# Unread TensorE products in front of the first merge's products and behind the scores of ten half units

## The chip, the cores and the metric

The kernel runs on one core of one Trainium2 chip. The metric is the device time of one execution in microseconds (us), lower is better. A core has TensorE (PE; the load of its stationary operand is listed apart, as PEld), VectorE (DVE), ScalarE (ACT), GpSimd (POOL) and queues that issue DMAs; SyncE's (SP) is the one used most here. Each engine works through its own queue in order; semaphores make one engine wait for another or for a DMA.

## The reference

One layer of a hybrid diffusion backbone on 1024 latent tokens and 256 context tokens of width 1024, in float32. What matters here, cut short:

```python
h  = rmsnorm(x, g_pre) * (1 + scale) + shift              # adaLN, likewise hc for the context
na_q, na_k, na_v, na_z, g_qkv, g_z, g_b, g_a = split(h @ w_in)
o_na = neighborhood_attention(...)                        # 8 heads, windows of 8 x 16 on a 16 x 64 grid, plus all context keys
...
# gated DeltaNet, 4 heads, both directions, in chunks:
a     = where(i > j, (kb @ k.T) * decay, 0)
t_inv = triangular_solve(eye + a, eye)                    # unit lower triangular inverse
u, w  = t_inv @ (v * beta), t_inv @ (kb * exp(gc))
state, o = scan(step, state0, ...)
y = concat(o_na * silu(na_z), o_g * silu(g_z)) @ w_out
x = x + gate * rmsnorm(y, g_post)
```

## The kernel before

Every projection `h @ w_in` is done as three products of rounded halves (`hh`, `hl` for the tokens, `wh`, `wl` for the weights), each 128 x 512 and eight deep in the width. A product that goes to a gate is called `pz` (lines L603, L607 and L608 of `mm_chan`), one that goes to a query or a key `pq` or `pk`. ScalarE and VectorE take the sum out of PSUM (`st_z` for a gate, L703 and L704) and SyncE's queue stores it (`z_dram`).

The triangular inverses of the DeltaNet chunks (128 x 128 per chunk, head and direction) are made in two steps. VectorE inverts the 32 x 32 diagonal blocks by substitution (`ab_vv`, L1255 and L1258) and they go to DRAM (`yd`). Then `inv_merge`, once per head, loads these blocks (`vl<-yd`, four DMAs) and the off-diagonal parts (`pmf<-pm_dram`, two DMAs, one per direction, `pm[0]` and `pm[1]` in the code), turns them with three transposes on VectorE in a row (`vx`, `vd`, `ld`, L1291 to L1293), and joins blocks of 32 to 64 and of 64 to 128 by small products on TensorE. The first of these small products of a head are the 40 of 32 x 32 for each stage named `tz` (L1305): they need `ld` and `pmf`. They are followed by `tu` (L1324), then 64 x 64 products (L1338, L1344, L1346), and the merged inverse goes to DRAM (`tm_dram`, L1351). There are two buffers of `vl`, and one `tm` buffer (`self.tms[2]`) serves every head in turn.

While the merges run, `phase_a2` feeds the projections that are still missing (`pz`, `pq`, `pk`) between the steps of the merges, with higher priorities for the merges. The order within each engine's queue is then chosen by a scheduler that runs a time model of the program when it is built: it decides how many `pz` products stand in front of the first `tz` product. TensorE itself takes its queue strictly in that order.

Then comes the neighbourhood attention with the DeltaNet scan beside it. The attention goes through 32 units (pair of heads, half of the rows, quarter of the columns), each with two half units, one per head (`hh`). A half unit is: `na_scores` (four products into one PSUM tile `sc`, L902 and L905; VectorE adds the bias and takes the minimum, L909; ScalarE exponentiates, L910), `na_turn` (five transposes on TensorE, L919 and L926, taken out by ScalarE) and, per unit, `na_values` (`po`, L937 and L942). The first four products and the scan's are chained by `self.pe`, so the scheduler keeps them in the order of the code. There is one `sc` buffer of 1024 columns, of which a half unit uses at most 640 (columns 128 to 768).

At the end the output projection (`py`, L1550 to L1552) writes `out`.

## Time and profile before

| what | value |
|---|---|
| median of the 3 runs shown | 854.17 us |
| these runs | 863.13, 847.94, 854.17 us |
| profiled execution, its own time | 848.82 us |
| its span (first to last instruction) | 847.1 us |
| TensorE busy | 814.2 us (96%), 6170 products |
| VectorE, ScalarE, GpSimd busy | 495.0, 418.0, 365.5 us |
| mean granted TensorE clock | 0.990 |

The profiled execution is one of the program's executions; its trace is what all views are taken from. "Busy" counts a product from its start to its modelled end, so products that overlap in the array make TensorE look full. The column PEclk in a view by stretches is the clock that TensorE was granted, 1.00 is full speed.

### The profile page before, as it was taken

The page shows a single profiled execution, that of the slowest core. Times are in us where ns is not written, and L with a number is a line of the kernel's source. Part 1 is how long each engine was busy: PE and PEld are TensorE (multiplying, and loading weights), DVE is VectorE, ACT ScalarE, POOL GpSimd, SP SyncE. Part 2 cuts the span into 40 slices and gives each one's busy share as a digit, 9 for nine tenths or more (in the row PEclk, how much of TensorE's full clock was granted, in tenths as well). Part 3 has the DMA queues.
Part 4 walks back from the last instruction along what each step waited for, and adds up shares of the span by engine and source line. Part 5 has one row for each costly group of instructions (what it writes and reads, how often), then busy time and mean ns, then how long its engine had stood idle before and what let it go on. Part 6 is the DMA issues. An engine that isn't in the chain of part 4 may idle for free.

```text
span 847.1 us, 16613 instructions
## 1 busy us (share of the span) xinstructions
PE 814.2 (96%) x6170; PEld 695.3 (82%) x6170; DVE 495.0 (58%) x988; ACT 418.0 (49%) x1097; POOL 365.5 (43%) x436
## 2 busy tenths in 40 slices
PE   8999999999999999988997999899999999999996
PEld 6688887888788878878985787799898989878885
DVE  4673455546456757699926955556566565743342
ACT  4472525654564664643214334566666666753211
POOL 0042221363482572555452103565757567835121
PEclk9999999999999999999998999999999999999999
DMA  9986442254626626733688579996967923234261
GB/s 332 341 305 213 136 138 90 79 180 161 162 75 227 197 69 230 218 110 102 202 241 239 166 223 293 392 306 181 313 186 257 250 97 128 87 125 137 99 199 50
DMA packets 86343, 159.67 MB, mean 188 GB/s; under 512 B 18405, under 2 KB 45750, under 8 KB 84086
## 3 DMA queue, kind: packets, MB, share of 16 engines
q1 hardware_dynamic: 78774, 144.94, 54.0%
q10 hardware_dynamic: 7488, 13.67, 5.5%
q8 instruction: 49, 0.80, 0.4%
q14 instruction: 32, 0.26, 0.1%
HBM read 109.51 MB, written 52.42 MB: 191 GB/s over the span
## 4 chain that ended last, share of the span: by engine, by line
PE 76%; DMA 9%; DVE 7%; POOL 3%; issue 2%; ACT 2%; SPq 0%; DVEq 0%; POOLq 0%; ACTq 0%
PE py L1550 4%; PE py L1552 3%; PE py L1551 3%; PE pz L607 3%; PE pz L608 3%; PE pz L603 3%; PE pa L1437 3%; DMA vl<-yd 2%; PE po L942 2%; PE po L937 2%; PE tr L926 2%; PE sc L905 2%; PE pa L1422 2%; PE pv L618 2%; PE pv L617 2%; PE pv L616 2%
## 5 line engine op out<-in xcount | busy, mean ns | idle before, releaser
L909 DVE CUSTOM_DVE_ANT_0 pt<-sc,gm 128x544 f32<-128x544 f32 (+1 forms) x64 | 49.4, 772 | 32.3 <-PE sc L905 28.6
L910 ACT ACTIVATE pt<-pt,nm 128x544 f32<-128x544 f32 (+1 forms) x64 | 50.5, 789 | 31.1 <-DVE nm L909 30.7
L893 POOL TENSOR_TENSOR gm<-gt,mk 128x288 f32<-128x288 f32 (+1 forms) x48 | 46.5, 972 | 21.8 <-DVE nm L909 18.6
L1412 POOL TENSOR_SCALAR kd<-kt,kd 128x128 f32<-128x128 f32 x72 | 42.7, 604 | 18.7 <-PE pa L1451 18.2
L1040 DVE SCALAR_TENSOR_TENSOR acc_v<-xp_v,cols,acc_v 128x1282 f32<-128x1282 f32 x16 | 33.1, 2068 | 26.9 <-ACT acc_v L1038 26.6
L1193 POOL TENSOR_SCALAR_AFFINE_SELECT qe<-qe 128x256 f32<-128x256 f32 x32 | 29.0, 907 | 39.8 <-DVE qe L1192 39.8
L1616 DVE TENSOR_TENSOR finv<-py,ggb 128x512 f32<-128x512 f32 (+1 forms) x17 | 10.7, 656 | 51.4 <-ACT finv L1615 43.0
L603 PE MATMUL pz<-hh,wh_gz 128*128 128x512 f32 x96 | 38.9, 405 | 0.0
L607 PE MATMUL pz<-hl,wh_gz 128*128 128x512 f32 x96 | 38.8, 405 | 0.0
L608 PE MATMUL pz<-hh,wl_gz 128*128 128x512 f32 x96 | 38.8, 404 | 0.0
L1174 ACT ACTIVATE em<-em,gc 128x128 f32<-128x128 f32 x80 | 25.5, 390 | 25.7 <-DMA em<-gc_dram 22.9
L618 PE MATMUL pv<-wl_nv,hh 128*128 128x264 f32 x104 | 30.5, 296 | 4.8 <-DVE wl_nv L586 4.8
L1189 DVE SCALAR_TENSOR_TENSOR pm<-pk,nsc,em 128x128 f32<-128x128 f32 x80 | 23.5, 342 | 18.5 <-PE pk L1182 14.6
L1418 POOL TENSOR_SCALAR vb<-v,beta 128x128 f32<-128x128 f32 x40 | 24.2, 606 | 23.0 <-DVE y L1424 13.1
L586 POOL TENSOR_TENSOR wl_gz<-wr_gz,wh_gz 128x512 fp32r<-128x512 f32 x12 | 15.5, 1290 | 37.3 <-ACT wh_gz L585 35.8
L926 PE MATMUL tr<-c,pt 128*96 128x128 f32 (+1 forms) x192 | 31.4, 273 | 0.0
L1454 DVE SCALAR_TENSOR_TENSOR s<-s,egl,pa 128x128 f32<-128x128 f32 x64 | 19.4, 342 | 20.1 <-PE pa L1451 20.1
L924 ACT COPY tcx<-tc 128x256 f32<-128x256 f32 x64 | 23.5, 367 | 15.1 <-PE tc L919 14.5
L928 ACT COPY tl<-tr 96x384 f32<-96x384 f32 (+1 forms) x64 | 30.5, 476 | 0.0
L617 PE MATMUL pv<-wh_nv,hl 128*128 128x264 f32 x104 | 30.0, 291 | 0.0
L616 PE MATMUL pv<-wh_nv,hh 128*128 128x264 f32 x104 | 29.2, 292 | 0.0
L1615 ACT ACTIVATE finv<-py 128x512 f32<-128x512 f32 x14 | 8.3, 598 | 38.7 <-PE py L1552 20.5
(469 smaller groups left out, 2859.3 us busy)
## 6 DMA issues: line engine op xcount, KB each, us to landing
wada<-in_w_ada SPq DMA_DIRECT2D x16, 512.0 KB
em<-gc_dram SPq DMA_DIRECT2D x20, 256.0 KB
pm_dram<-pm SPq DMA_DIRECT2D x20, 256.0 KB
tm_dram<-tm SPq DMA_DIRECT2D x8, 640.0 KB
kk<-qk_dram SPq DMA_DIRECT2D x16, 320.0 KB
tm<-tm_dram SPq DMA_DIRECT2D x4, 1280.0 KB
kq_dram<-kq SPq DMA_DIRECT2D x4, 1152.0 KB
kq<-kq_dram SPq DMA_DIRECT2D x4, 1152.0 KB
```

The costliest lines, as they stand in the source:

```text
L603: r = nc.tensor.matmul(ps, wh, xh, start=(k == 0 and first), stop=False)
L607: nc.tensor.matmul(ps, wh, xl, start=False, stop=False)
L608: nc.tensor.matmul(ps, wl, xh, start=False, stop=(k == KC - 1))
L616: nc.tensor.matmul(ps, xh, wh, start=(k == 0), stop=False)
L617: nc.tensor.matmul(ps, xl, wh, start=False, stop=False)
L618: nc.tensor.matmul(ps, xh, wl, start=False, stop=(k == KC - 1))
L893: r = nc.gpsimd.tensor_tensor(self.gm[hh][:, 384 - n:384].rearrange("p (n c r) -> p n c r", c=nco, r=4), gv, self.mk[:, mo:mo + n].rearran ...
L909: nc.vector.tensor_tensor_reduce(pt[:, 384 - n:], sc[:, 512 - n:768], gm[:, 384 - n:], -1.0, 3.0e38, ALU.add, ALU.min, nm)
L910: self.last_exp = nc.scalar.activation(pt[:, 384 - n:], pt[:, 384 - n:], AF.Exp, bias=nm, scale=-1.0, accum_out=sums[:, ct, hh:hh + 1]).in ...
L926: self.pe(nc.tensor.transpose(pl[:m, rc * P:(rc + 1) * P], pt[:, 384 + (rc - 3) * m:384 + (rc - 2) * m], self.ident))
L1412: r = nc.gpsimd.tensor_scalar(kd[d], kt_[:, t, :], self.kd[:, h, d, t:t + 1], None, ALU.mult)
L1550: nc.tensor.matmul(py, mh[:, tt], wh[:, nn], start=(k == W_ORDER[0]), stop=False)
```

## The change

A new function `hold` issues `n` products of 128 x 128 whose result nobody reads. It is called in two places:

- in `inv_merge`, for head 0 and direction 0 alone, in front of the 32 x 32 products: nine products that read `pm[1]` (so they wait for the DMA `pmf` of direction 1), then eight that read `vx` (so they wait for VectorE's first transpose). They write the PSUM tile that the small products then overwrite.
- in `na_scores`, for the first pair of heads and the first five units: two products of the identity by itself behind the four score products of each half unit, ten half units in all. They write columns 768 to 896 of the `sc` tile, which hold nothing. They are chained by `self.pe`.

```diff
+    def hold(self, dst, n, by=None):
+        w, x = by or (self.ident, self.ident)
+        for _ in range(n):
+            r = self.nc.tensor.matmul(dst, w, x, start=True, stop=True)
+            if not by:
+                self.pe(r)
...
                                      start=(i == 0), stop=(i == 1)))
+        if p == 0 and u < 5:
+            self.hold(sc[:, 768:896], 2)
...
             pz = ps.tile([P, 10, 32], F32, name=f"tz{h}_{d}", tag="ta", bufs=3)
+            if h == d == 0:
+                pzf = pz.rearrange("p t c -> p (t c)")[:, :P]
+                self.hold(pzf, 9, (self.ident[:96], pm[1][:96, 0, :]))
+                self.hold(pzf, 8, (self.ident, vx[:, :P]))
             for t in range(10):
```

The changed file has seven lines more above `na_scores` and up to thirteen more further down, so L905 becomes L912, L1305 becomes L1318 and L1351 becomes L1364. The new products all have line L750.

The scheduler places instructions anew from the first `hold` on. On TensorE, around the first merge, this stood there before (`pk` and `pz` are projections, `tz` is head 0's first stage; the numbers behind a name are those of buffers and views):

```order
L608 MATMUL pk_1_4656<-hh,wl_nk_4_4433 128x512
L603 MATMUL pz_0_4738<-hh,wh_gz_0_4727 128x512
L607 MATMUL pz_0_4738<-hl,wh_gz_0_4727 128x512
...
L608 MATMUL pz_0_4738<-hh,wl_gz_4_4734 128x512
L603 MATMUL pz_0_4738<-hh,wh_gz_4_4733 128x512
L1305 MATMUL tz_0_4491<-ld_4338,pmf_0_4330 32x32 x20
L1305 MATMUL tz_1_4514<-ld_4338,pmf_1_4332 32x32 x20
L607 MATMUL pz_0_4738<-hl,wh_gz_4_4733 128x512
```

and this stands there now:

```order
L608 MATMUL pk_1_4673<-hh,wl_nk_4_4433 128x512
L603 MATMUL pz_0_4755<-hh,wh_gz_0_4744 128x512
L750 MATMUL tz_0_4491<-pmf_1_4332,c_60 128x128 x9
L750 MATMUL tz_0_4491<-vx_4352,c_60 128x128 x8
L1318 MATMUL tz_0_4491<-ld_4338,pmf_0_4330 32x32 x20
L1318 MATMUL tz_1_4531<-ld_4338,pmf_1_4332 32x32 x20
L607 MATMUL pz_0_4755<-hl,wh_gz_0_4744 128x512
L608 MATMUL pz_0_4755<-hh,wl_gz_0_4745 128x512
```

Before, 19 `pz` products stood between the last `pk` and the first `tz`; now one does. The other 18 have moved behind head 0's `tz`, and the 17 unread products stand where they were.

On SyncE's queue, where the projections end and the attention begins, this stood there before (`kk` are loads of the attention's keys, `z_dram<-st_z` the stores of the last two gate tiles, `tm_dram_87` head 2's merged inverse, `zs` and `tm_5533` loads for the attention and the scan):

```order
L205 DMA kk_0_5465<-qk_dram 64x1280 x2
L705 DMA z_dram<-st_z_5373 128x512
L205 DMA kk_1_5474<-qk_dram 64x1280 x2
L705 DMA z_dram<-st_z_5461 128x512
L1351 DMA tm_dram_87<-tm_4336 128x1280
L1351 DMA tm_dram_87<-tm_4340 128x1280
L205 DMA zs_0_5517<-z_dram 128x512
```

and this stands there now:

```order
L205 DMA kk_1_5491<-qk_dram 64x1280 x2
L705 DMA z_dram<-st_z_5390 128x512
L1364 DMA tm_dram_87<-tm_4336 128x1280
L1364 DMA tm_dram_87<-tm_4340 128x1280
L705 DMA z_dram<-st_z_5478 128x512
L205 DMA zs_0_5534<-z_dram 128x512
```

Head 2's two stores stood behind the store of the last gate tile and now stand in front of it.

On TensorE, at the first scores (`sc_0_0` is the first half unit, `tz` and `tu` with these numbers are head 3's merge), this stood there before:

```order
L1346 MATMUL tu_15_5421<-z_5377,xo 64x64
L902 MATMUL sc_0_0_5521<-kk_0_5465,qh_0_5468 128x256
L902 MATMUL sc_0_0_5521<-kk_0_5465,ql_0_5471 128x256
L905 MATMUL sc_0_0_5521<-kk_0_5465,qh_0_5468 128x288
L905 MATMUL sc_0_0_5521<-kk_0_5465,ql_0_5471 128x288
L1305 MATMUL tz_0_5548<-ld_5138,pmf_0_5133 32x32 x20
L1305 MATMUL tz_1_5571<-ld_5138,pmf_1_5135 32x32 x20
```

and this stands there now:

```order
L608 MATMUL pz_1_5453<-hh,wl_gz_4_5361 128x512
L1318 MATMUL tz_0_5567<-ld_5155,pmf_0_5150 32x32 x20
L1318 MATMUL tz_1_5590<-ld_5155,pmf_1_5152 32x32 x20
...
L909 MATMUL sc_0_0_5538<-kk_0_5482,qh_0_5485 128x256
L909 MATMUL sc_0_0_5538<-kk_0_5482,ql_0_5488 128x256
L912 MATMUL sc_0_0_5538<-kk_0_5482,qh_0_5485 128x288
L912 MATMUL sc_0_0_5538<-kk_0_5482,ql_0_5488 128x288
L750 MATMUL sc_0_0_5538<-c_60 128x128 x2
```

The first scores stood in front of head 3's first stage and now stand behind it, with the two unread products behind them.

## The prediction

> **What bounds the kernel now.** I read the page's busy times first, then the chain of work that ended last, then what TensorE waited for.

> ```profile
> span 847.1 us, 16613 instructions
> PE 814.2 (96%) x6170; PEld 695.3 (82%) x6170; DVE 495.0 (58%) x988; ACT 418.0 (49%) x1097; POOL 365.5 (43%) x436
> PE 76%; DMA 9%; DVE 7%; POOL 3%; issue 2%; ACT 2%; SPq 0%; DVEq 0%; POOLq 0%; ACTq 0%
> PE tz L1305 <- DVE ld L1293: 5.6, 1, 5.6
> PE pv L618 <- DVE wl_nv L586: 4.8, 1, 4.8
> ```

> TensorE is busy for 96% of the span and carries 76% of the chain, so a microsecond taken from it, or handed to it while it has work queued, is mostly a microsecond of the end. Its longest single wait is 5.6 us in front of head 0's first small products (L1305), for `ld`. That is the place of the first edit. The two rows around it, and the first row behind the slow stretch, in order of time (start, duration):

> ```profile
> 443.15 0.41 PE L603 MATMUL pz<-hh,wh_gz 128*128 128x512 f32 x1
> 443.39 0.40 PE L607 MATMUL pz<-hl,wh_gz 128*128 128x512 f32 x1
> 447.35 0.40 PE L603 MATMUL pz<-hh,wh_gz 128*128 128x512 f32 x1
> 453.32 2.34 PE L1305 MATMUL tz<-ld,pmf 32*32 32x32 f32 x80 [5.58 <-DVE ld L1293]
> 455.59 0.80 PE L607 MATMUL pz<-hl,wh_gz 128*128 128x512 f32 x1
> 459.04 0.39 PE L603 MATMUL pz<-hh,wh_gz 128*128 128x512 f32 x1
> ```

> The 17 `pz` products from 443.39 to 447.35 start 3.96 / 17 = 0.233 us apart. Behind the wait, the eight from 455.59 to 459.04 start 3.45 / 8 = 0.431 us apart. The clock says why (columns: stretch, its length, PE busy, PEclk, DMA share, GB/s):

> ```profile
> 316.00:317.00 1.00, 0.96 (x7) 1.00 0.00 0
> 317.00:318.00 1.00, 0.00 (x0) 1.00 0.00 0
> 318.00:319.00 1.00, 0.11 (x1) 0.96 0.00 0
> 319.00:320.00 1.00, 1.00 (x5) 0.50 0.42 133
> 322.00:323.00 1.00, 1.00 (x5) 0.84 0.65 246
> 452.00:453.00 1.00, 0.00 (x0) 0.52 0.69 188
> 458.00:459.00 1.00, 1.00 (x4) 0.57 0.75 206
> 11.72:15.13 3.41, 1.83 (x13) 1.00 1.00 375
> 455.45:458.87 3.42, 3.42 (x16) 0.50 0.91 287
> 452.04:455.45 3.41, 2.13 (x80) 0.50 0.77 247
> ```

> After a wait the clock falls to 0.50. From the shares, it fell at 452.04 and came back at 458.86 (6.8 us), and in an earlier place fell at 318.92 and came back at 322.32 (3.4 us). That earlier fall followed an idle time of about 1.9 us, while a stretch of 3.41 us with TensorE 54% busy (11.72 to 15.13) brought none.

> **The change, part by part.** The sum is made against the profiled execution, 848.82 us.

> *Displaced products: +4.2.* Eighteen `pz` products that filled the time up to 447.6 now stand behind head 0's `tz`. Their time is 18 x 0.233 = 4.2 us, and `ld`, on which `tz` waits, comes when it came:

> ```profile
> 449.82 1.25 DVE L1291 STREAM_TRANSPOSE vx<-vl 128x1024 f32<-128x1024 f32 x1 [5.39 <-DMA vl<-yd]
> 452.43 0.83 DVE L1293 STREAM_TRANSPOSE ld<-vd 128x640 f32<-128x640 f32 x1
> ```

> The first transpose waits for a DMA, which the change leaves alone, so `tz` still starts at 453.3 and TensorE has 4.2 us more to do after it. Queued behind the new waits are these 18 products, then the tile's way out: ScalarE's and VectorE's `st_z` and the store on SyncE's queue.

> *The unread products: 0 here.* Fourteen products of 128 x 128 took

> ```profile
> 8.02 1.73 PE L162 MATMUL pv<-raw 128*128 128x128 f32 x14
> 447.42 1.52 SPq L1285 DMA_DIRECT2D vl<-yd  x3
> SPq L1285 <- DMA pmf<-pm_dram: 3.7, 2, 2.1
> ```

> 1.73 / 14 = 0.12 us each, so 0.24 at half the clock. The first nine wait for `pmf` of direction 1. The trace gives no landing times, but SyncE's queue waited twice for `pmf` before it went on with `vl` (the second row is the view of the queue from 447 on, the third covers 425 to 460), so I put that landing at 447.4. The nine then end by 449.6 at the latest, the eight start when `vx` is there (449.82 + 1.25 = 451.07) and end by 453.0 at half the clock. Both fit in front of 453.3: cost nothing. If `vx` comes late, `ld`, 2.2 us behind it, is late too, so the cover stays.

> *The clock: -1.2.* Before, the slow stretch costs twice. Eighty small products took 2.34 us (453.32), where 80 later ones take

> ```profile
> 525.88 1.45 PE L1305 MATMUL tz<-ld,pmf 32*32 32x32 f32 x80
> ```

> 1.45, so 0.9 us, and the eight `pz` 3.45 - 8 x 0.233 = 1.6 us: 2.5 in all. That bounds the gain (0 to 2.5). Now TensorE stands idle from 443.6 to 447.4, twice as long as the 1.9 us that brought a fall, so I expect the clock to fall still, one or two microseconds earlier. But the stretch from 452.04 to 455.45, 2.13 of 3.41 us busy before and not enough to bring the clock back (the next one, fully busy, was), gets up to 1 us of the eight in front, so the clock may come back one step of 3.4 us sooner. Where the steps lie can differ from one execution to the next, so I take the middle, 1.2.

> [...]

> *What later idle time gives back: -1.9.*

> ```profile
> 460.00:525.00 65.00, 63.80 (x946) 1.00 0.74 223
> 525.00:560.00 35.00, 32.49 (x501) 1.00 0.99 377
> PE tz L1338 <- DVE tm L1329: 1.5, 1, 1.5
> DVE tm L1329 <- DMA tm_dram<-tm: 1.6, 1, 1.6
> 525.15 0.33 SPq L705 DMA_DIRECT2D z_dram<-st_z  x1
> 525.57 0.88 SPq L1351 DMA_DIRECT2D tm_dram<-tm  x2
> ```

> Up to 525 TensorE is idle for 65.0 - 63.8 = 1.2 us, mostly small waits that lateness can swallow; I take 0.4 (0 to 1.2). From 525 to 560 it is idle for 2.5 us. 1.5 of them are one wait on VectorE, which itself waited 1.6 for head 2's store, and that store (525.57) stood in SyncE's queue behind the last gate tile's (525.15). In the new order it stands in front, so this wait should go: 1.5 (0 to 2.5). What is late next there is `st_z`, for which the first scores waited, and the moved `tz` of head 3 stands in that gap.

> *Twenty unread products behind scores: +2.0.* 20 x 0.12 = 2.4 us of TensorE.

> ```profile
> 525.18 0.39 PE L902 MATMUL sc<-kk,qh 128*128 128x256 f32 x1 [0.52 <-DVE st_z L704]
> 557.91 0.36 PE L902 MATMUL sc<-kk,qh 128*128 128x256 f32 x1
> DVE pt L909 <- PE sc L905: 13.3, 13, 2.4
> ```

> The ten half units' scores run from 525.18 to 557.91 (the tenth's). In that range the clock stays at 1.00, so there is nothing of the clock to win in this execution. VectorE waited for scores 13 times between 508 and 625 (third row). In the built program the score products themselves no longer signal; the second unread product carries the signal for VectorE. So where TensorE has work queued a pair delays it by 0.24 us, and where it waits for the chain scores, minimum, exponential, the pair lengthens that chain by the same 0.24. Only waits for something else hide it. Bounds 0 and 2.4; near the upper end, 2.0.

> **Sum:** 4.2 - 1.2 - 1.9 + 2.0 = +3.1, so 848.8 + 3.1 = 851.9 for an execution like the profiled one. The four known executions are 847.94, 848.82, 854.17 and 863.13; halfway between the inner two is 851.5, 2.7 above the profiled one, and the median shown is 5.4 above it. A new median of a few runs lies about where theirs does, so I add 2.7: **854.6 us**.

> **The rivals.**

> [...]

> *Nothing is given back (slower).* The displaced products are the price, at L750 on TensorE: if the clock comes back where it did and later waits are for work that TensorE itself delays, then 4.2 + 0 + 0 + 2.4 = +6.6, 855.4, as a median 858. It decides when the waits from 460 to 560 keep their sum of 3.7 us. For it: 230 us of unbroken TensorE work just before show how little slack there is. Against it: one of these waits has lost its cause.

> ```profile
> 80.00:310.00 230.00, 230.00 (x1228) 1.00 0.45 139
> ```

> *The change does nothing.* If the transition at 525 hangs on DMAs (share 0.99 there) and not on TensorE, lateness up to 3.7 us disappears in it and the pairs beside it: 848.8 ± 1, as a median 851.5.

> **How the numbers follow.** Chances: forecast 0.45, faster rival 0.2, nothing given back 0.2, nothing happens 0.15. On the profile's basis these reach from 846.8 to 855.4. The runs' own scatter, from 0.9 below the profiled execution to 5.4 above it without the highest, widens that: 847 to 862 us. Two per cent of this kernel is 17 us, about what a measurement of it can tell from no change, and no case reaches that; only the scatter that gave 863.13 can. So: faster by over 2% 0.02, within 2% 0.94, slower by over 2% 0.04.

> **What would show it.** In the changed trace: the nine products of L750 start at about 447.4 with some 3.8 us of idle time ahead of them, for a DMA; the eight at 451.1; `tz` at 453.3 as before; PEclk 0.50 in some stretch from 446 on and back to 1.00 by 455.5 to 459; the 18 `pz` behind it; the wait of 1.5 us for VectorE's `tm` (L1338 before, L1351 now) gone; each pair behind scores 0.24 us long. I am wrong if `pmf` lands before 444 (then the nine run at once and the longer wait is for `vx`), if `tz` starts elsewhere than near 453.3, or if the span beyond 560 changes its length by over 1 us.

## The result, and the profile after

| | before | after |
|---|---|---|
| median | 849.53 us (13 runs, 847.10 to 863.13) | 854.62 us (13 runs, 850.81 to 862.52) |
| profiled execution | 848.82, span 847.1 | 856.59, span 854.9 |

The ratio after to before is 1.0061 (95%: 1.0038 to 1.0084): some 5 us slower, 3 to 7. Here and below, a ratio leaves out the executions that took over 1.5% longer than the fastest one of the same kernel. The number forecast, 854.6, is the one measured. The working behind it is not: two of its terms were too small, by 1.9 and 2.5 us, a fall of the clock was missing, and what came back was twice what it said.

The page after, in the lines that were read before, and the two rows of TensorE's waits that are new (columns: us in total, times, longest us):

```profile
span 854.9 us, 16758 instructions
PE 825.3 (97%) x6244; PEld 708.2 (83%) x6244; DVE 491.3 (57%) x988; ACT 417.9 (49%) x1097; POOL 366.7 (43%) x436
PE 72%; DMA 10%; DVE 9%; POOL 3%; issue 2%; ACT 2%; SPq 1%; DVEq 0%; POOLq 0%; ACTq 0%
PE tz L750 <- DMA pmf<-pm_dram: 3.8, 1, 3.8
PE pos L1475 <- DMA qe<-qe_dram: 2.0, 1, 2.0
```

37 new products, 74 new records (6170 to 6244): **each unread f32 product is two records**. The 5.6 us wait for `ld` is gone, 3.8 us of waiting for `pmf` stand in its place, and a wait for the scan's `qe` came up later. At the merge, in order of time (start, duration), with VectorE's `ld` beside it:

```profile
448.39 4.21 PE L750 MATMUL tz<-pmf,c 96*128 96x128 f32 x18 [3.76 <-DMA pmf<-pm_dram]
452.39 2.90 PE L750 MATMUL tz<-vx,c 128*128 128x128 f32 x16
455.23 1.45 PE L1318 MATMUL tz<-ld,pmf 32*32 32x32 f32 x80
456.61 0.50 PE L607 MATMUL pz<-hl,wh_gz 128*128 128x512 f32 x1
452.54 0.84 DVE L1302 STREAM_TRANSPOSE ld<-vd 128x640 f32<-128x640 f32 x1
```

`ld` is there at 453.38 (453.26 before), but TensorE is still in the unread products and starts `tz` at 455.23. The nine take 4.0 us at half clock (448.39 to 452.39), 0.44 each. The clock, in its steps of 3.41 us (columns: stretch, its length, PE busy with the number of records, PEclk, DMA share, GB/s):

```profile
444.14:447.55 3.41, 0.48 (x3) 1.00 1.03 191
447.55:450.97 3.42, 2.58 (x12) 0.50 0.92 219
450.97:454.38 3.41, 3.41 (x18) 0.50 0.76 189
498.75:502.16 3.41, 3.41 (x105) 1.00 0.80 231
502.16:505.58 3.42, 3.42 (x9) 0.50 0.83 221
```

It falls at 447.55 and is back at 454.38, in time for `tz` (1.45 us) and all `pz` behind it. It falls once more at 502.16, behind a step that TensorE fills without a gap, but with 32 x 32 and 64 x 64 products of a later merge. The same products in before's profile brought no fall: there an edge of the steps, at 499.82, cut the sequence in two, and each of the two steps had products of 128 x 512 in it as well (496.41 to 499.82 and 499.82 to 503.23, both without a gap, in 94 and 51 records; PEclk 1.00 in both and in the step behind them).

From the first `pz` behind `tz` to the end in three stretches (to the last `pz`, on to the eleventh score, the rest), first before, then after:

```profile
455.59:523.37 67.78, 66.92 (x940) 0.98 0.75 229
523.37:561.91 38.54, 35.69 (x539) 1.00 0.97 361
561.91:847.10 285.19, 273.33 (x2158) 1.00 0.55 166
...
456.61:528.38 71.77, 71.38 (x980) 0.98 0.72 217
528.38:567.45 39.07, 38.18 (x559) 1.00 1.00 365
567.45:854.90 287.45, 273.62 (x2158) 0.99 0.55 162
```

After is 1.0 us late at the first `pz` behind `tz` (456.61 against 455.59), 5.0 late at the last one (71.77 - 67.78 = 4.0 more), 5.5 late at the eleventh score (39.07 - 38.54 = 0.5 more), and 7.8 at the end. The last 2.3 have the same 2158 products in them; 2.0 is the wait for `qe`.

### The profile page after: what moved, and what is told of

The parts are those of the page before. It is cut to its first block, busy times and chain, and to the rows that moved or that the text cites. A ratio compares the mean times of both kernels' runs of the same rounds, so it can differ in the third digit from the quotient of the medians.

```text
span 854.9 us, 16758 instructions
## 1 busy us (share of the span) xinstructions
PE 825.3 (97%) x6244; PEld 708.2 (83%) x6244; DVE 491.3 (57%) x988; ACT 417.9 (49%) x1097; POOL 366.7 (43%) x436
## 4 chain that ended last, share of the span: by engine, by line
PE 72%; DMA 10%; DVE 9%; POOL 3%; issue 2%; ACT 2%; SPq 1%; DVEq 0%; POOLq 0%; ACTq 0%
PE py L1563 4%; PE py L1565 3%; PE py L1564 3%; PE pz L607 3%; PE pz L608 3%; PE pz L603 3%; PE pa L1450 2%; PE po L951 2%; PE tr L935 2%; PE po L946 2%; PE sc L912 2%; DMA pm_dram<-pm 2%; DMA qe<-qe_dram 2%; DMA x<-in_x 2%; PE pa L1435 2%
## 5 line engine op out<-in xcount | busy, mean ns | idle before, releaser
L603 PE MATMUL pz<-hh,wh_gz 128*128 128x512 f32 x96 | 38.3, 399 | 0.0
L607 PE MATMUL pz<-hl,wh_gz 128*128 128x512 f32 x96 | 38.3, 399 | 0.0
L618 PE MATMUL pv<-wl_nv,hh 128*128 128x264 f32 x104 | 30.7, 298 | 4.8 <-DVE wl_nv L586 4.8
L586 POOL TENSOR_TENSOR wl_gz<-wr_gz,wh_gz 128x512 fp32r<-128x512 f32 x12 | 15.7, 1311 | 32.1 <-ACT wh_gz L585 28.3
```

Source lines behind the costliest of these rows:

```text
L603: r = nc.tensor.matmul(ps, wh, xh, start=(k == 0 and first), stop=False)
L607: nc.tensor.matmul(ps, wh, xl, start=False, stop=False)
L618: nc.tensor.matmul(ps, xh, wl, start=False, stop=(k == KC - 1))
```

## The experiments

Theory at the start: an f32 product is two records and takes 0.23 us at full clock, so the seventeen are late by 1.9 us and the pairs cost 4.4; the eighteen displaced `pz` cost 4.2; the clock gives 2.5 back. Rivals: the whole loss comes from the pairs, or from the merge part, or from the order into which the scheduler put everything behind it. Ratios are to before, timed beside each kernel; a profile is one execution. These runs were made on three chips, on two of which the median of before was 848.4 and 848.7 us. On the third, which ran the pairs without the seventeen, the second execution in before's order and before once more, it was 852.3. Lines of code are shortened to what they do.

### One part alone

The merge part without the pairs:

```diff
-        if p == 0 and u < 5:
-            self.hold(sc[:, 768:896], 2)
```

> The seventeen unread products in front of the first merge stay, the pairs behind the scores go. Theory (an f32 product of 128x128 is two passes and takes 0.23 us at full clock, 0.46 at half): the 17 end 1.9 us behind the landing of ld, eighteen pz are displaced (4.2 us), the clock gives back 2.5 us: 3 to 4 us slower than before (ratio 1.0035 to 1.005), and up to 1.7 us more where the later merge's small products fill a clock window of 3.4 us by themselves. Rival 1 (all of the loss comes from the pairs): ratio 1.000. Rival 2 (all of it comes from the merge, the pairs lie in idle time): the whole 1.006 of the change.

Measured: 1.0043 (1.0013 to 1.0073). As in the change, `tz` starts late, though by 0.8 us behind `ld` and not by 1.8, the eighteen follow, and the clock falls again at a later merge, here behind a step that is mostly idle:

```profile
446.93:453.76 6.83, 5.82 (x27) 0.50 0.91 207
467.41:470.82 3.41, 1.35 (x20) 1.00 0.49 135
470.82:477.65 6.83, 6.74 (x23) 0.50 0.48 150
```

So rival 1 falls; rival 2, all of it from the merge part (1.006), lies inside the interval. The pairs without the merge part:

```diff
-            if h == d == 0:
-                pzf = pz.rearrange("p t c -> p (t c)")[:, :P]
-                self.hold(pzf, 9, (self.ident[:96], pm[1][:96, 0, :]))
-                self.hold(pzf, 8, (self.ident, vx[:, :P]))
```

> The pairs behind the first ten scores stay, the seventeen products in front of the merge go; TensorE's other order and SP's are those of before. Theory (a pair takes 0.44 us, ten take 4.4): in the ten half units TensorE waits for some 1.1 us without the wait for tm, which the pairs fill, so 2 to 3.5 us slower (ratio 1.0025 to 1.004). Rival 1 (the pairs lie in idle time altogether): 1.000, with the tenth score at the same distance from the first as in before (32.7 us). Rival 2 (the pairs carry the whole loss): 1.006.

Measured: 1.0015 (0.9989 to 1.0041), which rules out that the pairs carry the whole loss, but cannot tell the theory from nothing. The profile can. The stretch from the last `pz` to the eleventh score, the tenth pair (four records) and what follows it:

```profile
523.30:564.84 41.54, 40.17 (x580) 1.00 0.99 353
560.99 0.61 PE L750 MATMUL sc<-c 128*128 128x128 f32 x4
561.52 0.66 PE L946 MATMUL po<-tcx,vcx 128*64 128x128 f32 x8
```

The last `pz` comes when it came before (523.30 against 523.37), the eleventh score 3.0 us later (41.54 us behind it instead of 38.54). Idle time shrinks from 38.54 - 35.69 = 2.85 us to 1.37, so the ten pairs take 3.0 + 1.5 = 4.5 us, 0.45 each, and a third of that is hidden.

### The order or the products

The two parts bring two things at once: products, and another order. To part them, every engine's queue was written out as it stands in one kernel and imposed on another: each instruction is made to follow its neighbour in that list, so that nothing but the products differs. The order of the change's merge part, with no unread product at all:

```diff
-                self.hold(pzf, 9, (self.ident[:96], pm[1][:96, 0, :]))
-                self.hold(pzf, 8, (self.ident, vx[:, :P]))
...
-    K(tc, I, out, dbg).run()
+    k = K(tc, I, out, dbg); k.run(); replay(k, QUEUES)     # QUEUES: those of the merge part alone
```

> No unread product at all; every engine's queue in the order that the merge part of the change brought (head 0's tz behind the first pz, with the transfers and the later merges as they stand there). Theory: the order is the loss. tz starts as in before, at half clock, eighteen pz come behind it (4.2 us, and up to 3.4 us more at half clock): ratio 1.004 to 1.008. Rival 1 (the order costs nothing, what counts is the time of the seventeen): 1.000. Rival 2 (the eighteen pz are given back by idle time later): 1.000 to 1.002.

Measured: 1.0155 (1.0120 to 1.0189), twice the upper end of what the theory gave for it. **The order alone costs 13 us; with its seventeen products in it, it costs 4.** The profile, of the slowest of six executions (867.86 us), shows where clock is lost:

```profile
448.67:462.32 13.65, 5.97 (x89) 0.50 0.87 243
530.59:534.00 3.41, 3.05 (x147) 1.00 1.00 393
534.00:561.31 27.31, 25.58 (x207) 0.50 1.00 395
```

Twice as long at half clock at the first merge as in the change, and then 27 us, eight steps, over the ten half units. A step of small products (3.05 us busy in 147 records) brings the fall. The following ones mix scores and transposes with products of 64 x 64 or 128 x 64, and the clock comes back behind the first one that has none of these (557.89 to 561.31). In the same order with the seventeen, the step that brought no fall there looks much the same:

```profile
532.26:535.68 3.42, 3.23 (x164) 1.00 0.97 360
535.68:563.00 27.32, 26.18 (x269) 1.00 1.00 399
```

What the seventeen, 80 us earlier, have to do with this step is not settled. The mean clocks of the other executions agree with the profiles, 0.966 to 0.978 here and 0.979 to 0.988 with the seventeen, so the lost clock is no accident of one trace; where it is lost, only the profiles show.

An order nearer to before's, in which only the eighteen `pz` are forced behind `tz`:

```diff
+    r = the second pz product: self.order(r, last tz product of head 0)     # and no hold()
```

> No unread products at all; only the order of the change: the eighteen pz stand behind head 0's tz instead of ahead of it. Theory: TensorE idles from about 444 to 453.4, the eighteen cost 4.2 us behind tz, and as the clock falls early and comes back only after tz, up to fifteen of them cost 0.23 us more: 4 to 6 us slower than before (ratio 1.005 to 1.007), above the merge alone, since there the clock was back for tz. Rival 1 (idle time later gives the displaced products back): ratio under 1.002. Rival 2 (the whole price of the merge part is the lateness of tz behind the unread products): 1.000.

Measured: 1.0074 (1.0030 to 1.0118), just above what was expected, but not for the reason given: five of the twelve executions took 850.6 to 854.3 us and seven 860.9 to 866.2, which the working of 4 to 6 us cannot make. The ratio has four of these seven, so it is too low if anything. The profiled one has the long stretch too:

```profile
532.32:559.63 27.31, 27.21 (x216) 0.50 1.00 395
```

Then the ten pairs in the change's order, without the seventeen:

```diff
-                self.hold(pzf, 9, (self.ident[:96], pm[1][:96, 0, :]))
-                self.hold(pzf, 8, (self.ident, vx[:, :P]))
...
+    k = K(tc, I, out, dbg); k.run(); replay(k, QUEUES)     # QUEUES: those of the change
```

> Every engine's queue in the order of the change, the ten pairs in their places, the seventeen products left out. In the same order without any unread product TensorE ran at half clock for 27 us of the ten half units, in the same order with the seventeen alone it did not. Theory (the pairs are what keeps a fallen clock from lasting there: a window must be nearly full of wide products to bring it back): no fall of more than two windows between 525 and 565, the fall at 447 to 461 stays (6.8 us lost), ratio 1.005 to 1.009. Rival (the pairs do not hold the clock, what matters is what the seventeen shift): half clock again over some 27 us, ratio 1.013 to 1.018.

Measured: 1.0064 (1.0032 to 1.0096), the theory's range. The clock still fell in the ten half units, but for four steps instead of eight:

```profile
530.97:534.38 3.41, 1.93 (x69) 1.00 0.90 270
534.38:548.03 13.65, 13.65 (x95) 0.50 1.00 402
```

My "no fall of more than two windows" was wrong. The queues of VectorE, GpSimd and SyncE are the same as in the kernel without any product, and of ScalarE's 953 instructions seven stand elsewhere. So the pairs win 0.6% (by the medians, 861.4 and 856.3 us, of two chips) to 0.9% (by the ratios, 1.0155 and 1.0064) where the seventeen are missing, and nothing that can be measured where these are there (1.0043 and 1.0061).

### The products in before's order

The seventeen put behind the nineteen `pz`, where `tz` stood before, the scheduler free in all else:

```diff
+    r = the nineteenth pz product: self.order(first unread product, r)     # no pairs
```

> No pairs; the seventeen unread products stand in TensorE's queue behind the nineteenth pz, where tz stood before, so that nothing is displaced. Theory: the nine find pmf landed and take 2.1 us at full clock from 447.5, the eight start when vx comes (451.1) and end at 453.0, before ld; tz starts as in before, and the clock is not lost, since no idle stretch is over 1.6 us: 2 to 2.5 us faster than before (ratio 0.997 to 0.998). Rival 1 (the unread products do not hold the clock): 1.000, with tz and eight pz at half clock. Rival 2 (the transfers move again with the order, and a wait for one of them takes the gain): 1.000 or above, with a new DMA wait on TensorE.

Measured: 1.0128 (1.0082 to 1.0174). At the merge the theory was right to some tenths of a microsecond, and the forecast of a gain was wrong:

```profile
448.17 2.17 PE L750 MATMUL tz<-pmf,c 96*128 96x128 f32 x18
450.90 2.05 PE L750 MATMUL tz<-vx,c 128*128 128x128 f32 x16 [0.56 <-DVE vx L1300]
453.15 1.45 PE L1318 MATMUL tz<-ld,pmf 32*32 32x32 f32 x80 [0.20 <-DVE ld L1302]
508.03:511.44 3.41, 1.04 (x36) 1.00 1.16 255
511.44:525.10 13.66, 12.85 (x149) 0.50 0.88 274
```

The nine take 0.24 us each at full clock, `tz` starts on time and at full clock; but the scheduler placed the later merges anew, a step with 1.04 us of work at 508 was followed by 13.7 us of half clock, and the first score came 15.5 us late (540.72). TensorE's new waits on the way are for ScalarE and VectorE (1.6 and 1.5 us the longest), none for a DMA, as one rival had it. So once more with before's queues imposed whole, and the seventeen in front of `tz`:

```diff
-        if p == 0 and u < 5:
-            self.hold(sc[:, 768:896], 2)
...
+    k = K(tc, I, out, dbg); k.run(); replay(k, QUEUES, held)     # QUEUES: those of before; held: the seventeen
```

> No pairs. Every engine's queue stands in the order of before, instruction by instruction; the seventeen unread products are put in right ahead of head 0's tz, behind the nineteen pz, and nothing else moves. Theory (the loss of the merge part is the order, not the products): they run at full clock from 447.5, wait 0.5 us for vx, end by 453, tz starts at 453.2 and takes 1.45 us instead of 2.34, the next eight pz run at full clock: 2.5 us faster (ratio 0.997), if no clock window falls later. Rival 1 (the unread products are the loss): 1.003 or above. Rival 2 (a later start on the clock's grid of 3.41 us makes the small products of a later merge fill a window): 0.999 to 1.003, with a new fall of the clock between 460 and 530.

Measured: 1.0023 (0.9995 to 1.0051): not the 0.997 of the theory. Both rivals, no gain and a loss of 1.003, lie inside the interval. The profiled execution, 847.49 us, does at the merge what was expected:

```profile
446.72 2.17 PE L750 MATMUL tz<-pmf,c 96*128 96x128 f32 x18
451.27 1.45 PE L1318 MATMUL tz<-ld,pmf 32*32 32x32 f32 x80 [0.19 <-DVE ld L1302]
537.17:540.58 3.41, 2.80 (x29) 1.00 1.01 419
540.58:544.00 3.42, 3.42 (x19) 0.51 0.99 414
```

The clock stays up at the merge and the first score is 2.5 us early (522.72), but the first `pz` was early by 0.9 already (442.29 against 443.15), so 1.6 are won between the two. One step of half clock at 540 takes up to 1.7 back. A second execution of the same file:

> The seventeen products in the order of before, no pairs, once more. Theory: no fall at the wait for ld in any execution, but falls between 460 and 560 that the first profile had only once (at 540), and a time that follows them: 847 to 849 with one, 852 to 855 with three or four windows. Rival (the loss of its median is somewhere else than in the clock): a time over 850 with the clock lost in one window or none between 440 and 600.

It took 853.12 us with no fall at all between 440 and 840, which is the rival's case; executions of before on this chip with as high a mean clock (0.988 to 0.990) took 847.5 to 852.1:

```profile
458.00:525.00 67.00, 65.83 (x938) 1.00 0.78 235
525.00:565.00 40.00, 36.67 (x548) 1.00 0.96 352
PE tz L1351 <- issue: 2.0, 1, 2.0
```

The first `pz` was already 3.8 us late there (446.95 against 443.15). The wait of a merge's `tz`, behind GpSimd's `tm`, is 2.0 (1.5 in before), and a wait of 1.9 for `qe` is new. From the first `pz` to the first score it is 79.95 us here and 80.43 in the other profile, 82.03 in before: 2.1 and 1.6 us won. Why the median has none of it is not settled: such waits and the place of the falls differ from one execution to the next by more than that. The whole change in before's order:

```diff
+    k = K(tc, I, out, dbg); k.run(); replay(k, QUEUES, held)     # QUEUES: those of before; held: the seventeen and the twenty
```

> The whole change, the seventeen and the ten pairs, with every engine's queue in the order of before: only the scheduler's reordering is taken out of the change. Theory: the clock gives 2.5 us, the pairs take 4.2 us of which 1.7 lie in idle time: ratio 1.000. Rival 1 (the products alone make the loss, the order none of it): 1.006 as in the change. Rival 2 (the pairs are hidden, the clock gives 2.5): 0.997.

Measured: 1.0085 (1.0061 to 1.0109). All expectations were too low, and the parts (1.0023 and 1.0015) add up to less, by hardly more than the intervals allow. At the eleventh score the profile is at 568.55, 6.6 us late:

```profile
DVE pt L918 <- PE sc L750: 10.7, 7, 5.0
PE tz L1351 <- issue: 2.3, 1, 2.3
```

From 525 to 560 VectorE waits 10.7 us for the pairs' signal (8.1 in the change), and the wait of a later merge's `tz`, 0.2 us in the change's order of the transfers, is back with 2.3. The clock adds two steps at half speed (469.48 and 537.75), up to 3.4 us. So taking the reordering out of the change does not take its loss out; whether the change's order suits the pairs better than before's is not shown, since the intervals overlap (1.0061 and 1.0085).

### What a product costs, and what it buys

The change with its own queues imposed, and 64 columns per unread product:

```diff
-            r = self.nc.tensor.matmul(dst, w, x, start=True, stop=True)
+            r = self.nc.tensor.matmul(dst[:, :64], w, x[:, :64], start=True, stop=True)
```

> The change as it is, in its own order, but every unread product reads 64 columns instead of 128. Theory (a product's time goes by its columns, twice over for f32): 0.12 us each at full clock, 0.24 at half, as the prediction priced them at 128 columns: the seventeen end about when ld comes, tz is at most 0.5 us late instead of 1.9, a pair takes 0.23 us, ten 2.3 instead of 4.2: some 3 us under the change, ratio 1.002 to 1.004. Rival (the price is one per instruction, whatever its columns): 1.006, tz 1.9 us late.

Measured: 1.0071 (1.0048 to 1.0093), with `tz` 1.6 us behind `ld`: the rival. The products and the loads of their stationary operand here, the same loads in the change, and a product of two columns in before:

```profile
447.22 4.10 PE L750 MATMUL tz<-pmf,c 96*128 96x64 f32 x18 [2.37 <-DMA pmf<-pm_dram]
454.66 2.35 PE L1318 MATMUL tz<-ld,pmf 32*32 32x32 f32 x80
L750 PEld LDWEIGHTS tz<-pmf,c 96*128 96x128 f32 x18 | 3.9, 330 | 2.8 <-DMA pmf<-pm_dram 2.8
446.80:460.45 13.65, 13.23 (x122) 0.50 0.92 265
450.21:453.63 3.42, 3.42 (x18) 0.50 0.75 214
...
L750 PEld LDWEIGHTS tz<-pmf,c 96*128 96x128 f32 x18 | 3.9, 332 | 4.2 <-DMA pmf<-pm_dram 4.2
...
17.02 1.02 PE L162 MATMUL pa<-c,rows 128*128 128x2 f32 x8
```

Nine take 4.10 us as they took 4.21 with twice the columns, and eighteen loads of the stationary operand take 3.9 us in both kernels. Eight records of two columns took 1.02 us at full clock, 0.13 each, about as much as those of 128 columns; eighty of 32 x 32 took 1.45, 0.02 each, so it is not one price per record either. What fits is that the load of the stationary operand sets the pace. And though TensorE is busy for 13.23 of 13.65 us, the clock stays down for four steps instead of two, so `tz` runs at half clock. A step filled without a gap by 18 records of 64 columns left it at half (450.21 to 453.63), where 18 of 128 columns brought it back in the change (450.97 to 454.38) and in the merge part alone (450.35 to 453.76). **From 128 columns to 64 the time is the same (4.21 and 4.10 us), but the clock seems to count them;** the narrow ones have one profile.

### Before once more

The kernel before, with blank lines so that its lines have the numbers of the change; no instruction differs.

> The kernel before once more (blank lines only). Theory (the clock is judged in windows of 3.41 us whose start against the program differs from run to run): the fall at the wait for ld is there again, the others may lie elsewhere or be missing, and the time follows the clock lost: 846 to 849 with 10 us lost or less, 852 to 858 with 15 to 25. Rival (the falls belong to places in the program): the same places as before, to within 3.5 us.

It took 853.9 us, against 848.8 for the execution that the prediction read; the median on this chip is 852.3:

```profile
450.35:457.18 6.83, 6.73 (x91) 0.50 0.90 311
498.14:501.55 3.41, 3.41 (x9) 0.50 0.94 272
532.27:549.33 17.06, 17.06 (x114) 0.50 1.01 417
```

The theory: the fall at the merge is there again, and two new ones, at the same small products (498) and at the start of the half units (532). The time follows the clock lost: of 29 executions of before on one chip those with a mean clock of 0.988 and more took 846.4 to 848.8 us, the one with 0.969 took 858.8; on this chip 0.988 and more took 847.5 to 852.1, and 0.973 took 860.8. So a long fall can come in before too. The change's order without products has the low clock in all six executions, and in its profiles with either kind of unread product the long fall is shorter or missing.

## Why the prediction was right, and where not

Its terms for the profiled execution, up to the eleventh score, and what the traces show:

| term | predicted | measured |
|---|---|---|
| eighteen `pz` behind `tz` | +4.2 | +4.2 (18 x 0.233, all behind `tz`) |
| seventeen unread products | 0 | +1.9 (`tz` at 455.23, not 453.3) |
| the clock at the merge | -1.2 | -2.5 (`tz` 1.45 us, no slow `pz`) |
| the clock elsewhere | none | +1.7 (the fall at 502: nine `pk` of 128 x 512) |
| twenty products behind scores | +2.0 | +4.5 (ten pairs of 0.45) |
| given back | -1.9 | -4.3 (the remainder) |
| sum | +3.1 | +5.5 |

- **Where the working failed: the price of an unread product.** The row of 14 records in 1.73 us was read as fourteen products; they were seven (the code issues 6, 7, 7 and 6 of them, the trace has 52 records), each two records. The same ratio stood in `tz`: 40 products in the order, 80 records in the row. "0.12 us each" was 0.24, "0.24 at half the clock" 0.44. With that price the seventeen need 6.8 us from 448.39 (the clock is back for the last few), "both fit in front of 453.3" was false, and the pairs cost twice their term. About 1 us of the lateness is another cause: SyncE's queue went on with `vl` behind `pmf` at 448.36, not at 447.42 as in before, so the nine started 1.0 us later than forecast. With `pmf` there at 447.94 and `ld` at 453.93, in the merge part alone, the same seventeen made `tz` 0.8 us late and not 1.8; at 0.24 at half clock they would have fitted in both. What these traces show is two records and two loads of the stationary operand for each product (18 of either for the nine), and no more can be seen in them.
- **The clock.** That it would fall all the same, and be back sooner, was right (454.38, not 458.86). But it fell 4.5 us earlier (447.55, not 452.04), where one or two were forecast, and stayed down for two steps as before. It was back in time for `tz`, behind the step that 18 records of the unread products filled without a gap (3.41 of 3.41 us busy): as I read it, the dear price of the first term paid for the second. That the clock would not fall at all, for which the faster rival and the 846.8 at the foot of the range stand, did not come: PEclk was 0.50 from 447.55 to 454.38. Where the steps lie did differ from one execution to the next (edges at 452.04 in before's first profile and at 450.35 in its second). The missing term was the second fall: that one can come behind a step without a gap (498.75 to 502.16, 3.41 us busy) was in no row of the one trace read.
- **Given back.** The wait for `tm` went as said (1.5 to 0.2). Idle time up to the eleventh score shrank by 0.5 (67.78 - 66.92 = 0.86 to 0.39) and 1.96 us (2.85 to 0.89), 2.4 together. The other 1.9 stay unassigned: TensorE's busy time in these two stretches rose by 6.9 us, where the terms add up to 8.8 (4.2 - 1.6 + 1.7 + 4.5; the 1.6 is what the slow `pz` had cost). Twenty 64 x 64 products of a merge (`tu`) moved from the second stretch into the first, where they may overlap more with wide products; that is not shown.
- **The median.** The profile's difference is 7.8 us, of which 2.0 is one wait for `qe` that other kernels show too, before among them in its second profile (0.6). The measured difference of the medians is 5.1. The 2.7 that I added for the runs' scatter belonged to a median of 854.17 of three runs; over 13 runs before's is 849.53. So +3.1 was 2 us short, +2.7 was 2 too many, and the number is right by that luck. Two of the prediction's own signs of being wrong came: `tz` did not start near 453.3, and the span behind the eleventh score grew by 2.3 us.
- **The rivals.** "Nothing is given back" has the sum (+6.6) that the profile came nearest to, with the wrong mechanism, since 4.3 came back; "the change does nothing" and the faster one are excluded by the interval.
- **What the prediction never asked** is what the order alone does. It took the displaced products as 4.2 us and the unread ones as nearly free; the runs say that the order without them is 13 us, and that they are worth some 9 us inside it (1.0155 to 1.0043). That is why the change costs so little, not why it costs: with before's order imposed, the whole change costs 1.0085.

The stretches at half clock behind 440 us are one step of 3.41 us long or a whole number of them: one in the change (502.16 to 505.58), two in before (452.04 to 458.87, 6.83 us), four in the pairs without the seventeen (13.65), five in before's second profile (17.06) and eight in the order without products (27.31). How much of the step ahead of a fall was idle differs: all of it in before (448.63 to 452.04) and in its second profile (446.94 to 450.35), while steps with 0.48 (the change, 444.14 to 447.55), 1.35 (the merge part alone), 1.93 (the pairs without the seventeen) and 2.80 us busy (before's order) and, with small products, one busy for all of its 3.41 us (the change, 498.75 to 502.16) were followed by falls as well.

## What to carry to other kernels

Before a filler product is priced, count the records that one of them makes, in a place of the trace where the program says how many were issued; its price may be that of loading its stationary operand, so a narrower one need not be cheaper, and it may hold the clock less (here nine of 64 columns took 4.10 us and nine of 128 took 4.21, the eighteen loads 3.9 us in both, and the clock was down for four steps with the narrow ones and for two with the others). A filler that is put into a scheduled program changes the order of everything behind it, and here the order by itself cost 13 us where the filler could win 2.5: part the two by imposing the old queues before judging either. And where executions of one kernel differ by more than the term in question, one profile is one draw: take a second of the kernel before, before arguing from what is not in the first.
